# Seven products of quarters for eight in the first MLP product of a transformer block

## The chip, the cores and the metric

The kernel runs on one core of one Trainium2 chip. The metric is the device time of one execution in microseconds, the median of several runs; a profiled execution gives the span from the first to the last instruction and the work of every engine: TensorE (PE, with its weight loads PEld), VectorE (DVE), ScalarE (ACT), GpSimd (POOL) and SyncE (SP), which issues the DMA transfers.

## The reference

A residual block over 512 tokens of width 1024: a gated linear recurrence and a differential attention run side by side on the same normed input, are merged and projected, and an MLP of width 4096 with a squared ReLU follows. All data are fp32. What matters here is the end:

```python
x = x + merged @ w_out[l]
h2 = rms_norm(x, norm2_g[l])
x = x + jnp.square(jax.nn.relu(h2 @ w_mlp1[l])) @ w_mlp2[l]
return rms_norm(x, normf_g)
```

`rms_norm` divides every token by the root of its mean square plus 1e-6 and multiplies by a gain per channel. `w_mlp1` is 1024 x 4096, `w_mlp2` 4096 x 1024.

## The kernel before

Activations lie transposed: 128 channels on the partitions, 512 tokens along the free dimension, so that 1024 channels are eight tiles (index `k` or `m`). Each fp32 operand is split into a high part (a cast to fp32r, on ACT) and a low part (the remainder, on DVE). `Build.mm` makes one block of 128 output channels from 8 tiles of k, each with three matmuls (high by high, high by low, low by high; lines 153 to 155): 24 matmuls of 512 columns into one PSUM bank.

Weights come in chunks of 128 x 1024, two to a DMA of 1 MB (`raw`, two buffers, issued on SP). `chunk_plan` writes their order out. `Build.emit_chunk` splits a chunk (lines 117 and 118) into the buffers `whi` and `wlo`, four of each; `Build.chunk` keeps three to four chunks ahead. A program places the instructions in each engine's queue at compile time, by their order in the source and by when their inputs should be ready; each engine then runs its queue in order.

The stages: values and other input projections, with attention and recurrence between them; the merge; the output projection with the residual (eight blocks, line 620 adds the residual, line 231 splits x times gain into the next product's operands); norm 2 (`token_rinv` sums the squares over channels by matmuls with a column of ones, line 245, takes the root and the reciprocal; `bcast_rinv` spreads it over the partitions by matmuls with an identity, line 256); then the MLP by quarters of its width:

```python
    mlp1(0)
    for qq in range(NQ - 1):
        mlp1(qq + 1)
        mlp2(qq)
```

`mlp1` makes eight blocks of the first product. Line 639 reads each from PSUM, clips it at zero and multiplies by the token scale; line 644 squares it into the high part, lines 645 and 646 give the low part. `mlp2` makes eight blocks of the second product from one quarter and line 653 adds each to the residual. The last quarter of the second product runs by halves of the tokens (256 columns), and line 672 adds; the final norm of each half ends with line 683 and the output transfers.

## Time and profile before

| | us |
|---|---|
| median of 3 runs (lowest, highest) | 901.84 (901.81, 902.35) |
| span of the profiled execution | 900.2 |
| PE busy in the span | 888.8 |
| DVE busy | 510.7 |
| ACT busy | 395.3 |

The runs' times and the span come from different executions; the profiled execution's own device time is not given beside its span. PE's busy time counts overlapping matmuls once, and the ends of matmuls are modelled, so the price of a matmul is read from the distance of two starts rather than from a duration.

### The profile page before, as it was taken

To read this page: it belongs to the slowest core of one execution; us is meant where nothing else is said; L and a number is where in the kernel's file an instruction comes from. 1 tells how busy PE (TensorE), PEld (TensorE's weight loads), DVE (VectorE), ACT (ScalarE), POOL (GpSimd) and SP (SyncE) were. 2 spreads that over 40 slices of the span, in tenths; PEclk is the share of its full clock that TensorE was granted. 3 is DMA by queue.
4 is the path that set the end of the run, shared out by engine and by line. 5 is a ranking of instruction groups with operands and counts; after the bars stand their busy time and mean duration, and the time that the engine had idled before them with its cause. 6 is when DMAs were issued, how large, how long until landed. Compare 5 with 4: busy or idle time off the path is not lost.

```text
span 900.2 us, 10638 instructions
## 1 busy us (share of the span) xinstructions
PE 888.8 (99%) x4209; PEld 720.1 (80%) x4209; DVE 510.7 (57%) x796; ACT 395.3 (44%) x658; POOL 0.3 (0%) x5
## 2 busy tenths in 40 slices
PE   9999999999999999999999999999999999999995
PEld 7887787777877788888888888888888888888995
DVE  7777698787887765333334555555335534555332
ACT  7544767857858973222223342222122212223232
POOL 0000000000000000000000000000000000000000
PEclk9999999999999999999999999999999999999998
DMA  8433123132323022222522222222222222225011
GB/s 279 171 125 114 59 71 129 59 111 83 109 70 109 13 82 94 93 94 94 187 93 94 94 95 93 94 94 94 94 94 94 94 94 93 94 94 175 13 48 48
DMA packets 20738, 88.49 MB, mean 98 GB/s; under 512 B 3024, under 2 KB 6352, under 8 KB 11728
## 3 DMA queue, kind: packets, MB, share of 16 engines
q1 hardware_dynamic: 20688, 87.81, 28.6%
q8 instruction: 33, 0.54, 0.2%
q14 instruction: 17, 0.14, 0.0%
HBM read 81.51 MB, written 2.10 MB: 93 GB/s over the span
## 4 chain that ended last, share of the span: by engine, by line
PE 97%; ACT 1%; DVE 1%; DMA 1%; SPq 0%; issue 0%; DVEq 0%; ACTq 0%
PE pmm L153 29%; PE pmm L154 28%; PE pmm L155 28%; PE psc L320 2%; PE pmm L320 2%; PE psc L408 2%; PE pmm L443 2%; PE ptr L431 1%; DMA L<-xT 1%; PE psc L504 1%; PE psc L506 0%; PE ptr L472 0%; PE psc L505 0%; PE psc L405 0%; PE ptr L245 0%; PE ptr L256 0%
## 5 line engine op out<-in xcount | busy, mean ns | idle before, releaser
L117 ACT CAST whi<-raw 128x1024 fp32r<-128x1024 f32 (+1 forms) x136 | 139.3, 1025 | 373.6 <-PE pmm L154 298.9
L153 PE MATMUL pmm<-X,whi 128*128 128x512 f32 x584 | 232.9, 399 | 0.0
L154 PE MATMUL pmm<-X,whi 128*128 128x512 f32 x584 | 230.7, 395 | 0.0
L155 PE MATMUL pmm<-X,wlo 128*128 128x512 f32 x584 | 230.7, 395 | 0.0
L118 DVE TENSOR_TENSOR wlo<-raw,whi 128x1024 fp32r<-128x1024 f32 (+1 forms) x136 | 161.8, 1191 | 75.0 <-ACT whi L117 74.5
L153 PEld LDWEIGHTS pmm<-X,whi 128*128 128x128 f32 x584 | 109.9, 188 | 29.2 <-issue 2.6
L155 PEld LDWEIGHTS pmm<-X,wlo 128*128 128x128 f32 x584 | 109.9, 188 | 25.8
L154 PEld LDWEIGHTS pmm<-X,whi 128*128 128x128 f32 x584 | 109.9, 188 | 25.3 <-issue 0.4
L639 DVE SCALAR_TENSOR_TENSOR tmp<-pmm,up 128x512 f32<-128x512 f32 x32 | 22.1, 691 | 68.7 <-PE pmm L155 68.7
L653 DVE TENSOR_TENSOR E<-pmm,E 128x512 f32<-128x512 f32 x24 | 16.6, 691 | 74.7 <-PE pmm L155 74.7
L213 ACT ACTIVATE B<-psc,nb 128x128 f32<-128x128 f32 (+3 forms) x64 | 33.2, 523 | 27.1 <-DVE nb L413 27.0
L213 ACT ACT_TABLE_LOAD x32 | 41.1, 1283 | 1.1 <-DVE nb L413 0.5
L155 PE MATMUL pmm<-B,wlo 128*128 128x512 f32 x96 | 38.0, 395 | 0.0
L155 PE MATMUL pmm<-V,wlo 128*128 128x512 f32 x96 | 37.9, 395 | 0.0
L153 PE MATMUL pmm<-B,whi 128*128 128x512 f32 x96 | 37.9, 395 | 0.0
L153 PE MATMUL pmm<-V,whi 128*128 128x512 f32 x96 | 37.9, 395 | 0.0
L154 PE MATMUL pmm<-B,whi 128*128 128x512 f32 x96 | 37.9, 395 | 0.0
L154 PE MATMUL pmm<-V,whi 128*128 128x512 f32 x96 | 37.9, 395 | 0.0
L155 PE MATMUL pmm<-R,wlo 128*128 128x512 f32 (+1 forms) x96 | 34.2, 356 | 0.0
L155 PE MATMUL pmm<-Q,wlo 128*128 128x512 f32 (+1 forms) x96 | 34.2, 356 | 0.0
L154 PE MATMUL pmm<-R,whi 128*128 128x512 f32 (+1 forms) x96 | 34.2, 356 | 0.0
L154 PE MATMUL pmm<-Q,whi 128*128 128x512 f32 (+1 forms) x96 | 34.2, 356 | 0.0
(232 smaller groups left out, 1411.4 us busy)
## 6 DMA issues: line engine op xcount, KB each, us to landing
raw<-wts SPq DMA_DIRECT2D x70, 1024.0 KB, 4.8
rot<-B SPq DMA_DIRECT2D x64, 64.0 KB, 2.0
L<-xT SPq DMA_DIRECT2D x8, 256.0 KB, 5.3
raw<-wts SPq DMA_DIRECT2D x8, 256.0 KB, 5.4
E<-xT SPq DMA_DIRECT2D x8, 256.0 KB, 4.5
out<-E SPq DMA_DIRECT2D x6, 256.0 KB, 2.5
tmp<-gates SPq DMA_DIRECT2D x8, 128.0 KB, 4.7
out<-E SPq DMA_DIRECT2D x4, 128.0 KB, 1.9
```

The lines of the kernel that those rows point to most:

```text
L117: nc.scalar.copy(hf[:, s], raw[:, s])
L118: nc.vector.tensor_tensor(lf[:, s], raw[:, s], hf[:, s].bitcast(F), op=ALU.subtract)
L153: nc.tensor.matmul(ps, hi[:, k], xh[k], start=(k == 0), stop=False)
L154: nc.tensor.matmul(ps, hi[:, k], xl[k], start=False, stop=False)
L155: nc.tensor.matmul(ps, lo[:, k], xh[k], start=False, stop=(k == KT - 1))
L213: ins = A.activation(*args, **kw).ins
L320: TE.matmul(pvs[half][i], xs[q][:, i * P:(i + 1) * P], (hv, lv)[wi][:, q % 2], start=(q == 0 and n == 0), stop=(q == KT - 1 and n == 2))
L408: TE.matmul(sc[:, m, :n], l[rows, 0, i * P:n], r[rows, 1, :n], start=(g == 0), stop=(g == 2))
L431: TE.transpose(pt[:, j], p[:, j * P:(j + 1) * P], ident)
L443: TE.matmul(po[:, i], pdT[:, j], v[j][:, h * P:(h + 1) * P], start=(j == 0), stop=(j == i))
L639: V.scalar_tensor_tensor(z, pz, 0.0, rb2, op0=ALU.max, op1=ALU.mult)
L653: V.tensor_tensor(x2[m], pz, x2[m], op=ALU.add)
```

## The change

The first product is taken in units. A unit makes two blocks of 128 output channels that lie 512 apart, for all tokens, as a product of 2 x 2 quarters: the channels of the input in two halves, the tokens in two halves, the output channels in two blocks. Strassen's scheme in Winograd's form makes it from seven products of quarters instead of eight. Each is 4 tiles of k, three matmuls each, with 256 columns: 12 matmuls, 84 a unit, into four PSUM banks (`BX`, `BY`, `BR`, `BZ`), three of which take a second product on top of the first. The seven weight operands ("pieces" of 128 x 512) are the four quarters or their sums, made by DVE and then split by ACT and DVE; the seven activation operands are made once, in the output projection's loop. Since sums of quarters are taken over tokens and channels, the token scale of norm 2 no longer stands between product and ReLU: the operands carry only a scale from norm 1's sums (`isz`), the residual is multiplied by the rest (`sig2`) ahead of the second product, and the final norm's epsilon becomes one per token (`eps4`). The squares of norm 2 are added on GpSimd.

Weights of the MLP come in units of 1 MB, one for the seven pieces of a "one" unit (first product) or the four pieces of a "two" unit (two blocks of the second product, four tiles of k each). A ring of eight pieces takes the place of the four chunk buffers; `use` makes the piece seven ahead. `mlp_order` gives four "one" units of the first quarter, and then "one" of the next quarter and "two" of this one in turn. The last quarter's eight chunks are held as before. The output projection goes over its blocks in the order 0, 4, 1, 5, 2, 6, 3, 7. The core of the diff:

```diff
+def mlp_order():
+    order = [("one", 0, i) for i in range(4)]
     for q in range(NQ):
-        if q + 1 < NQ:
-            for f in range(8):
-                plan.append(("w_mlp1", ((q + 1) * 8 + f) * P, 0))
-        for m in range(KT):
-            plan.append(("w_mlp2", m * P, q * D))
-    return plan
+        for i in range(4):
+            if q + 1 < NQ:
+                order.append(("one", q + 1, i))
+            order.append(("two", q, i))
+    return order
...
+    RING = 8
+    def plan_pieces(self):
+        self.units = mlp_order()
+        self.pieces = []
+        self.first = []
+        for u, (kind, q, i) in enumerate(self.units):
+            self.first.append(len(self.pieces))
+            if kind == "one":
+                self.pieces += [(u, j) for j in range(7)]
+            elif q < NQ - 1:
+                self.pieces += [(u, j) for j in range(4)]
+        self.ring_h, self.ring_l = [], []
+        self.piece, self.made = {}, 0
+        self.raw_u = {}
+        self.sums = {}
+    def load_unit(self, u):
+        if u < len(self.units) and u not in self.raw_u:
+            raw = self.t("raw", (P, 4, T), bufs=2)
+            self.nc.sync.dma_start(raw.rearrange("p c f -> p (c f)"), self.a["wts"][self.mlp0 // 2 + u])
+            self.raw_u[u] = raw
+    def split_to(self, src, hi, lo):
+        self.nc.scalar.copy(hi, src)
+        self.nc.vector.tensor_tensor(lo, src, hi.bitcast(F), op=ALU.subtract)
+    def make_piece(self):
+        V, n = self.nc.vector, self.made
+        u, j = self.pieces[n]
+        self.load_unit(u)
+        self.load_unit(u + 1)
+        raw = self.raw_u[u]
+        blk = [raw[:, i] for i in range(4)]
+        if self.units[u][0] == "one":
+            if j == 0:
+                s1 = self.sums[u] = self.t("pT", (P, T))
+                V.tensor_tensor(s1, blk[2], blk[3], op=ALU.add)
+                V.tensor_tensor(blk[2], blk[2], blk[0], op=ALU.add)
+            elif j == 1:
+                V.tensor_tensor(blk[0], blk[0], self.sums[u], op=ALU.add)
+            elif j == 6:
+                V.tensor_tensor(blk[1], blk[1], blk[0], op=ALU.add)
+            src = (blk[0], blk[0], blk[2], self.sums[u], blk[1], blk[3], blk[1])[j]
+        else:
+            src = blk[j]
+        s, e = n // 2 % (self.RING // 2), n % 2
+        if n < self.RING and e == 0:
+            self.ring_h.append(self.t("whi", (P, 2, T), FR, bufs=4))
+            self.ring_l.append(self.t("wlo", (P, 2, T), FR, bufs=4))
+        hi, lo = self.ring_h[s][:, e], self.ring_l[s][:, e]
+        self.split_to(src, hi, lo)
+        self.piece[n] = [x.rearrange("p (k m) -> p k m", m=P) for x in (hi, lo)]
+        self.made += 1
+    def make_until(self, n):
+        while self.made < min(n, len(self.pieces)):
+            self.make_piece()
+    def use(self, n):
+        self.make_until(n + self.RING)
+        return self.piece.pop(n)
+    def mm4(self, out, w, xs, first, last):
+        nc = self.nc
+        for k, (xh, xl) in enumerate(xs):
+            for g, (l, r) in enumerate(((w[0], xh), (w[0], xl), (w[1], xh))):
+                nc.tensor.matmul(out, l[:, k], r, start=(first and k == 0 and g == 0),
+                                 stop=(last and k == 3 and g == 2), skip_group_check=True)
...
-    def token_rinv(parts, sl=range(4)):
+    def token_sums(parts, sl=range(4)):
         pc = ps("tr", (P, T))
         for i in sl:
             for n, sq in enumerate(parts):
                 TE.matmul(pc[:, i:i + 1], sq[:, i * P:(i + 1) * P], ones[:, 0:1],
                           start=(n == 0), stop=(n == len(parts) - 1))
-        r = t("rcol", (P, 4))
-        s = slice(sl[0], sl[-1] + 1)
-        act(r[:, s], pc[:, s], AF.Sqrt, scale=1.0 / D, bias=eps1)
-        V.reciprocal(r[:, s], r[:, s])
-        return r
+        return pc
...
-    # ---- residual and norm 2 ----
-    x2, x2p = [], []
-    x2h, x2l = [], []
+    b.plan_pieces()
+    isz = t("isz", (P, 4))
+    V.reciprocal(isz, size1)
+    r1b = t("up0")
+    bcast_rinv(isz, r1b)
+    x2, x2p = [None] * KT, [None] * (KT // 2)
+    th = [t(f"X{2 * k}", (P, 4, H2), FR) for k in range(4)]
+    tl = [t(f"X{2 * k + 1}", (P, 4, H2), FR) for k in range(4)]
+    b2h = [t(f"L{k}", (P, 2, T), FR) for k in range(2)]
+    b2l = [t(f"L{k + 2}", (P, 2, T), FR) for k in range(2)]
+    b1h, b1l = t("S0", (P, 4, H2), FR), t("S1", (P, 4, H2), FR)
     ssq = t("up1")
-    for m in range(KT):
-        if m % 2 == 0:
-            xp = t(f"E{m // 2}", (P, 2, T))
-            x2p.append(xp)
-        xk = xp[:, m % 2]
+    for n, m in enumerate(OUT_ORDER):
+        k = m % 4
+        if n > 4:
+            b.make_until(2 * (n - 4))
+        if x2p[m // 2] is None:
+            x2p[m // 2] = t(f"E{m // 2}", (P, 2, T))
+        xk = x2[m] = x2p[m // 2][:, m % 2]
         nc.sync.dma_start(xk, a["xT"][m])
         po = b.proj(mh, ml)
         V.tensor_tensor(xk, po, xk, op=ALU.add)
-        x2.append(xk)
-        hi, lo = pair(f"X{m}")
-        split_scaled(xk, col(C_G2, m), hi, lo)
-        x2h.append(hi)
-        x2l.append(lo)
-        add_squares(ssq, xk, m == 0)
-    rcol = token_rinv([ssq])
-    rb2 = t("up0")
-    bcast_rinv(rcol, rb2)
-    # ---- MLP ----
-    fq = {}
-    def mlp1(qq):
-        out = []
-        for f in range(8):
-            pz = b.proj(x2h, x2l)
-            z = t("tmp", bufs=2)
-            V.scalar_tensor_tensor(z, pz, 0.0, rb2, op0=ALU.max, op1=ALU.mult)
-            if qq % 2 == 0:
-                hi, lo = pair(f"V{f}" if f < 4 else f"B{f - 4}")
+        if m < 4:
+            xs = t(f"V{k}", (P, 2, T))
+        V.scalar_tensor_tensor(xs[:, m // 4], xk, col(C_G2, m), r1b, op0=ALU.mult, op1=ALU.mult)
+        if n == 0:
+            A.activation(ssq, xk, AF.Square)
+        else:
+            sq = t("tmp", bufs=2)
+            A.activation(sq, xk, AF.Square)
+            nc.gpsimd.tensor_tensor(ssq, ssq, sq, op=ALU.add)
+        if m >= 4:
+            q4 = xs.rearrange("p a (c f) -> p (a c) f", c=2)
+            b.split_to(q4[:, 0], b1h[:, k], b1l[:, k])
+            tt = t(f"B{k}", (P, 4, H2))
+            V.tensor_tensor(tt[:, 0:3:2], q4[:, 0:2], q4[:, 1:4:2], op=ALU.subtract)
+            V.tensor_tensor(tt[:, 1], tt[:, 0], q4[:, 3], op=ALU.add)
+            V.tensor_tensor(tt[:, 3], q4[:, 2], tt[:, 1], op=ALU.subtract)
+            b.split_to(tt, th[k], tl[k])
+            b.split_to(xs[:, 1], b2h[k // 2][:, k % 2], b2l[k // 2][:, k % 2])
+    b.make_until(b.RING)
+    pc = token_sums([ssq])
+    sig2 = t("sig2", (P, 4))
+    V.tensor_scalar(sig2, pc[:, :4], 1.0 / D, EPS, op0=ALU.mult, op1=ALU.add)
+    V.tensor_tensor(sig2, sig2, isz, op=ALU.mult)
+    V.tensor_tensor(sig2, sig2, isz, op=ALU.mult)
+    eps4 = t("eps4", (P, 4))
+    V.tensor_tensor(eps4, sig2, sig2, op=ALU.mult)
+    V.tensor_scalar(eps4, eps4, EPS, None, op0=ALU.mult)
+    sg2b = t("up0")
+    bcast_rinv(sig2, sg2b)
+    for xp in x2p:
+        V.tensor_tensor(xp, xp, sg2b.unsqueeze(1).to_broadcast([P, 2, T]), op=ALU.mult)
+    xc = {
+        "b11": [(b1h[:, k], b1l[:, k]) for k in range(4)],
+        "b21": [(b2h[k // 2][:, k % 2, :H2], b2l[k // 2][:, k % 2, :H2]) for k in range(4)],
+        "b22": [(b2h[k // 2][:, k % 2, H2:], b2l[k // 2][:, k % 2, H2:]) for k in range(4)],
+    }
+    for j in range(4):
+        xc[f"t{j + 1}"] = [(th[k][:, j], tl[k][:, j]) for k in range(4)]
+    banks = [ps("sc", (P, 2, T), bufs=2) for _ in range(2)]
+    BX, BY, BR, BZ = (banks[n // 2][:, n % 2, :H2] for n in range(4))
+    fq = {q: [None] * KT for q in range(NQ)}
+    def f_split(q, f, z, lo_half):
+        if q % 2 == 0:
+            hi, lo = pair(f"V{f}" if f < 4 else f"B{f - 4}")
+        else:
+            hi, lo = pair(f"R{f}" if f < 4 else f"Q{f - 4}")
+        A.activation(z[:, lo_half:], z[:, lo_half:], AF.Relu)
+        A.activation(hi, z, AF.Square)
+        A.activation(z, z, AF.Square)
+        V.tensor_tensor(lo, z, hi.bitcast(F), op=ALU.subtract)
+        fq[q][f] = (hi, lo)
...
+    def one(u, q, i):
+        n = b.first[u]
+        z0 = t("up2" if i % 2 == 0 else "rot", bufs=1 + i % 2)
+        z1 = t("up3" if i % 2 == 0 else "rot", bufs=1 + i % 2)
+        b.mm4(BX, b.use(n), xc["b11"], True, True)
+        uu = t("tmp", (P, H2), bufs=2)
+        A.copy(uu, BX)
+        b.mm4(BY, b.use(n + 1), xc["t2"], True, True)
+        V.tensor_tensor(uu, BY, uu, op=ALU.subtract)
+        b.mm4(BR, b.use(n + 2), xc["t3"], True, True)
+        V.tensor_tensor(z1[:, H2:], BR, uu, op=ALU.add)
+        b.mm4(BZ, b.use(n + 3), xc["t1"], True, True)
+        V.tensor_tensor(z1[:, H2:], z1[:, H2:], BZ, op=ALU.subtract)
+        b.mm4(BX, b.use(n + 4), xc["b21"], False, True)
+        A.activation(z0[:, :H2], BX, AF.Relu)
+        b.mm4(BR, b.use(n + 5), xc["t4"], False, True)
+        V.tensor_tensor(z1[:, :H2], BR, uu, op=ALU.add)
+        b.mm4(BZ, b.use(n + 6), xc["b22"], False, True)
+        V.tensor_tensor(z0[:, H2:], BZ, uu, op=ALU.subtract)
+        f_split(q, i + 4, z1, 0)
+        f_split(q, i, z0, H2)
+    def two(u, q, i):
+        n = b.first[u]
+        for c in range(2):
+            m = 2 * i + c
+            pz = ps("mm", bufs=3)
+            for h in range(2):
+                b.mm4(pz, b.use(n + 2 * c + h), fq[q][4 * h:4 * h + 4], h == 0, h == 1)
+            V.tensor_tensor(x2[m], pz, x2[m], op=ALU.add)
...
+    def hold(u, i):
+        b.load_unit(u)
+        b.load_unit(u + 1)
+        for c in range(2):
+            e = 2 * i + c
+            if e < 4:
+                hi, lo = t(f"X{2 * e}", (P, KT, P), FR), t(f"X{2 * e + 1}", (P, KT, P), FR)
             else:
-                hi, lo = pair(f"R{f}" if f < 4 else f"Q{f - 4}")
-            A.activation(hi, z, AF.Square)
-            V.tensor_tensor(z, z, z, op=ALU.mult)
-            V.tensor_tensor(lo, z, hi.bitcast(F), op=ALU.subtract)
-            out.append((hi, lo))
-        fq[qq] = ([o[0] for o in out], [o[1] for o in out])
-    def mlp2(qq):
-        for m in range(KT):
-            pz = b.proj(*fq[qq])
-            V.tensor_tensor(x2[m], pz, x2[m], op=ALU.add)
-    mlp1(0)
-    for qq in range(NQ - 1):
-        mlp1(qq + 1)
-        mlp2(qq)
-    # ---- last quarter, by halves of the tokens, and the final norm ----
-    wl = []
+                hi, lo = t("whi", (P, KT, P), FR, bufs=4), t("wlo", (P, KT, P), FR, bufs=4)
+            b.split_to(b.raw_u[u][:, 2 * c:2 * c + 2], *(x.rearrange("p (c k) m -> p c (k m)", c=2) for x in (hi, lo)))
+            last_chunks.append((hi, lo))
+    held = 0
+    for u, (kind, q, i) in enumerate(b.units):
+        if kind == "one":
+            one(u, q, i)
+        elif q < NQ - 1:
+            two(u, q, i)
+            if q == NQ - 2 and i >= 2:
+                hold(len(b.units) - 4 + held, held)
+                held += 1
+    while held < 4:
+        hold(len(b.units) - 4 + held, held)
+        held += 1
...
-        rcol = token_rinv([ssq, sq], tk)
+        c = slice(2 * half, 2 * half + 2)
+        pc = token_sums([ssq, sq], tk)
+        rcol = t("rcol", (P, 4))
+        V.scalar_tensor_tensor(rcol[:, c], pc[:, c], 1.0 / D, eps4[:, c], op0=ALU.mult, op1=ALU.add)
+        act(rcol[:, c], rcol[:, c], AF.Sqrt)
+        V.reciprocal(rcol[:, c], rcol[:, c])
```

## Rows read from the trace of the kernel before

**Rows 1.** The page, busy time of each engine, share and instructions.

```profile
PE 888.8 (99%) x4209; PEld 720.1 (80%) x4209; DVE 510.7 (57%) x796; ACT 395.3 (44%) x658; POOL 0.3 (0%) x5
```

**Rows 2.** The page, chain that ended last, by engine.

```profile
PE 97%; ACT 1%; DVE 1%; DMA 1%; SPq 0%; issue 0%; DVEq 0%; ACTq 0%
```

**Rows 3.** Windows: stretch, length, busy us per engine (instructions), TensorE clock, DMA.

```profile
483.10:528.00 44.90, 44.90 (x194) 36.07 (x193) 24.78 (x31) 17.10 (x24) 0.00 (x0) 1.00 0.26 94
528.00:842.50 314.50, 314.50 (x1360) 253.94 (x1359) 154.73 (x183) 83.28 (x97) 0.00 (x0) 1.00 0.28 97
842.50:889.20 46.70, 46.70 (x399) 46.62 (x398) 16.01 (x35) 15.24 (x32) 0.00 (x0) 1.00 0.07 24
889.20:900.20 11.00, 1.82 (x14) 1.46 (x12) 3.13 (x7) 1.19 (x3) 0.00 (x0) 0.69 0.29 96
```

**Rows 4.** Timeline, DVE, first product: start us, duration us, instruction [idle before].

```profile
602.55 0.69 DVE L639 SCALAR_TENSOR_TENSOR tmp<-pmm,up 128x512 f32<-128x512 f32 x1 [2.11 <-PE pmm L155]
603.45 1.23 DVE L118 TENSOR_TENSOR wlo<-raw,whi 128x1024 fp32r<-128x1024 f32 x1 [0.20 <-ACT whi L117]
604.59 0.69 DVE L645 TENSOR_TENSOR tmp<-tmp 128x512 f32<-128x512 f32 x1
605.31 0.69 DVE L646 TENSOR_TENSOR Q<-tmp,Q 128x512 fp32r<-128x512 f32 x1
608.13 0.69 DVE L639 SCALAR_TENSOR_TENSOR tmp<-pmm,up 128x512 f32<-128x512 f32 x1 [2.13 <-PE pmm L155]
```

**Rows 5.** Timeline, DVE, last quarter.

```profile
845.93 0.42 DVE L672 TENSOR_TENSOR E<-pmm,E 128x256 f32<-128x256 f32 x1 [0.73 <-PE pmm L155]
...
851.56 0.42 DVE L672 TENSOR_TENSOR E<-pmm,E 128x256 f32<-128x256 f32 x1 [1.48 <-PE pmm L155]
```

**Rows 6.** Groups, weight loads: busy us, mean ns | idle before.

```profile
L154 PEld LDWEIGHTS pmm<-X,whi 128*128 128x128 f32 x584 | 109.9, 188 | 25.3 <-issue 0.4
...
L153 PEld LDWEIGHTS pmm<-R,X 128*128 128x128 f32 x32 | 6.0, 188 | 0.0
```

**Rows 7.** Timeline, DVE, runs of unrelated operations in the value stage.

```profile
35.77 4.91 DVE L316 TENSOR_TENSOR L<-L,up 128x512 f32<-128x512 f32 x8 [0.59 <-ACT up L260]
...
43.45 3.39 DVE L231 SCALAR_TENSOR_TENSOR X<-L,small,X 128x512 fp32r<-128x512 f32 x5
```

**Rows 8.** Timeline, the end of the kernel, DVE.

```profile
891.49 0.17 DVE L250 RECIPROCAL rcol<-rcol 128x2 f32<-128x2 f32 x1 [1.66 <-ACT rcol L213]
...
892.46 2.54 DVE L683 TENSOR_TENSOR E<-E,ptr 128x256 f32<-128x256 f32 x5 [0.80 <-PE ptr L256]
```

**Rows 9.** Groups by form, ACT: busy us, mean ns | idle before.

```profile
L117 ACT CAST whi<-raw 128x1024 fp32r<-128x1024 f32 x128 | 134.5, 1051 | 373.5 <-PE pmm L154 298.9 <-issue 64.5 <-PE pmm L155 4.8
...
L674 ACT ACTIVATE tmp<-E 128x256 f32<-128x256 f32 x14 | 5.8, 418 | 24.5 <-DVE E L672 24.5
...
L644 ACT ACTIVATE V<-tmp 128x512 fp32r<-128x512 f32 x8 | 5.0, 628 | 1.0 <-DVE tmp L639 1.0
...
L117 ACT CAST whi<-raw 128x512 fp32r<-128x512 f32 x8 | 4.9, 606 | 0.1
```

**Rows 10.** Timeline, PE, after the output projection.

```profile
531.75 0.99 PE L245 MATMUL ptr<-ones,up 128*128 128x1 f32 x8
532.60 0.48 PE L154 MATMUL pmm<-X,whi 128*128 128x512 f32 x1
...
534.78 1.05 PE L256 MATMUL ptr<-ident,rcol 128*128 128x128 f32 x8
535.59 0.47 PE L154 MATMUL pmm<-X,whi 128*128 128x512 f32 x1
```

**Rows 11.** Timeline, DVE, end of the output projection.

```profile
522.63 0.69 DVE L620 TENSOR_TENSOR E<-pmm,E 128x512 f32<-128x512 f32 x1 [2.27 <-PE pmm L155]
...
528.23 0.69 DVE L620 TENSOR_TENSOR E<-pmm,E 128x512 f32<-128x512 f32 x1 [2.27 <-PE pmm L155]
```

**Rows 12.** The page, DMA issues: KB each, median us to landing.

```profile
raw<-wts SPq DMA_DIRECT2D x70, 1024.0 KB, 4.8
```

More of the change, by code (lines that the diff above doesn't have):

```diff
@@ L34 @@
 NSMALL = 89
+OUT_ORDER = (0, 4, 1, 5, 2, 6, 3, 7)
+H2 = T // 2
 def chunk_plan():
@@ L52, in chunk_plan @@
             plan.append((kind, m * P, 0))
-    for m in range(KT):
+    for m in OUT_ORDER:
         plan.append(("w_out", m * P, 0))
-    for f in range(8):
-        plan.append(("w_mlp1", f * P, 0))
-    for q in range(NQ):
-        if q + 1 < NQ:
-            for f in range(8):
-                plan.append(("w_mlp1", ((q + 1) * 8 + f) * P, 0))
-        for m in range(KT):
-            plan.append(("w_mlp2", m * P, q * D))
-    return plan
+    for kind, q, i in mlp_order():
+        if kind == "one":
+            for f in (i, i + 4):
+                plan.append(("w_mlp1", (q * 8 + f) * P, 0))
+        else:
+            for m in (2 * i, 2 * i + 1):
+                plan.append(("w_mlp2", m * P, q * D))
+    return plan
+def mlp_order():
+    order = [("one", 0, i) for i in range(4)]
+    for q in range(NQ):
+        for i in range(4):
[3 more added lines that the diff above has]
+    return order
 def merge_order():
@@ L82, in __init__ @@
         self.nchunks = len(chunk_plan())
+        self.mlp0 = self.nchunks - 2 * len(mlp_order())
         self.split = {}
@@ L127, in wslot @@
             return "E0", "E1", 1
-        e = c - (self.nchunks - 8)
-        if 0 <= e < 4:
-            return f"X{2 * e}", f"X{2 * e + 1}", 1
         return "whi", "wlo", 4
@@ L136, in chunk @@
         ahead = 4 if c + 4 < self.P1_END else 3
-        if c >= self.nchunks - 8 - 4:
-            ahead = 7
-        while self.emitted < min(c + 1 + ahead, self.nchunks):
+        while self.emitted < min(c + 1 + ahead, self.mlp0):
             self.emit_chunk(self.emitted)
@@ L193, in block_kernel @@
     nc.sync.dma_start(ident, a["ident"])
+    size1 = t("size1", (P, 4))
     ones = t("ones", (P, 1))
@@ L308, in block_kernel @@
                 if half == 1 and k == 1:
-                    rcol = token_rinv([ssq])
+                    pc = token_sums([ssq])
+                    rcol = t("rcol", (P, 4))
+                    act(rcol, pc[:, :4], AF.Sqrt, scale=1.0 / D, bias=eps1)
+                    V.reciprocal(rcol, rcol)
+                    act(size1, pc[:, :4], AF.Sqrt, scale=1.0 / D, bias=ones)
                     v_store(0)
@@ L650, in mlp2 @@
-    def mlp2(qq):
-        for m in range(KT):
-            pz = b.proj(*fq[qq])
-            V.tensor_tensor(x2[m], pz, x2[m], op=ALU.add)
-    mlp1(0)
-    for qq in range(NQ - 1):
-        mlp1(qq + 1)
-        mlp2(qq)
-    wl = []
+        if m < 4:
[7 more added lines that the diff above has]
+            nc.gpsimd.tensor_tensor(ssq, ssq, sq, op=ALU.add)
@@ new lines, in block_kernel @@
+    b.make_until(b.RING)
+    pc = token_sums([ssq])
+    sig2 = t("sig2", (P, 4))
[9 more added lines that the diff above has]
+        V.tensor_tensor(xp, xp, sg2b.unsqueeze(1).to_broadcast([P, 2, T]), op=ALU.mult)
@@ new lines, in f_split @@
+    def f_split(q, f, z, lo_half):
+        if q % 2 == 0:
+            hi, lo = pair(f"V{f}" if f < 4 else f"B{f - 4}")
+        else:
+            hi, lo = pair(f"R{f}" if f < 4 else f"Q{f - 4}")
[25 more added lines that the diff above has]
+        f_split(q, i, z0, H2)
@@ L662, in block_kernel @@
+    held = 0
+    for u, (kind, q, i) in enumerate(b.units):
+        if kind == "one":
+            one(u, q, i)
[7 more added lines that the diff above has]
+        held += 1
     ssq = t("up1")
-    fh, fl = fq[NQ - 1]
-    H2 = T // 2
     for half in range(2):
@@ L667, in block_kernel @@
         for m in range(KT):
-            if half == 0:
-                wl.append(b.next())
+            hi, lo = last_chunks[m]
             pz = ps("mm", bufs=3)
-            b.mm(pz[:, s], wl[m], [f[:, s] for f in fh], [f[:, s] for f in fl])
+            for h in range(2):
+                b.mm4(pz[:, s], (hi[:, 4 * h:4 * h + 4], lo[:, 4 * h:4 * h + 4]),
+                      [(fh[:, s], fl[:, s]) for fh, fl in fq[NQ - 1][4 * h:4 * h + 4]], h == 0, h == 1)
             V.tensor_tensor(x2[m][:, s], pz[:, s], x2[m][:, s], op=ALU.add)
```

4 lines of the change are left out of this document (2 added, 2 removed).

## The prediction

> **What bounds the kernel now.** I read the busy totals first: TensorE (PE) is busy for 99% of the span, VectorE (DVE) for 57%, ScalarE (ACT) for 44% [rows 1]. A busy total alone can mislead where matmuls overlap, so the chain of waits comes second: 97% of what ended last is PE work [rows 2]. Third come the stages [rows 3]. Output projection, first and second product together, and last quarter have no PE gap, at a granted clock of 1.00 (the 2.4 GHz level). The middle stage, 528.0 to 842.5 us, holds the first product and three quarters of the second. DVE works for 154.7 of its 314.5 us. So PE time saved there shortens the kernel, as long as DVE and ACT can feed and empty the new products.
>
> PE's price is read from its readers' rhythm. In the first product the reader of each block starts at 602.55 and 608.13: 24 matmuls of 512 columns in 5.58 us, 0.2325 each [rows 4]. In the last quarter readers start at 845.93 and 851.56 with one between: 48 matmuls of 256 columns in 5.63 us, 0.1173 each [rows 5]. Half the columns cost half the time, plus 1%. This settles whether half-width products can pay at all.
>
> **The change part by part, on PE.** Before, two blocks of the first product are 48 matmuls: 48 x 0.2325 = 11.16 us. After, the same two blocks are seven products of 12 matmuls with 256 columns: 84 x 0.1173 = 9.85. The saving is 1.31 us a unit, over 16 units 20.9 us. The second product keeps 24 matmuls of 512 columns per block and the last quarter its 384 of 256. Added is one broadcast of the per-token scale, as long as the one in the trace, 534.78 to 535.59: **+0.8** [rows 10]. The token sums and the other broadcast stay.
>
> **Weights on DVE and ACT.** A "one" unit makes seven pieces of 512 columns. Its DVE work is 7 subtractions, 4 sums, 5 PSUM reads of 256 and 2 subtractions for f: 13 operations of 512 and 5 of 256. Eight unrelated operations of 512 took 4.91 us, the last one 0.69 in full: 0.60 from start to start [rows 7]. For 1024 it is 1.14 (603.45 to 604.59) [rows 4]. Five at the end took 2.54, of which two of 256 come to 0.33 each [rows 8]. The unit is 13 x 0.60 + 5 x 0.33 = 9.45 us of DVE beside 9.85 of PE. A "two" unit asks DVE for 6 x 0.60 = 3.6 beside 48 x 0.2325 = 11.16. So a pair is 13.05 of 21.0, and the eight-piece ring has the whole "two" unit to refill. I take **+0.5** for the 12 pairs; the bounds are 0 and 7 (one operation of 0.6 late in each).
>
> ACT, at full durations: 7 casts of 0.61, 5 operations of 0.63 and 3 of 0.42 make 8.7 us a unit [rows 9]. It is hidden under PE's 9.85; in the stretch below that cover is thin.
>
> **The stretch with no "two" unit.** The order begins with five "one" units. Here DVE has no slack, and leftovers come first. From the end of the output projection until the fifth unit's last piece is made, DVE must do: the last chunk's add, scale and split (0.60 + 0.66 + 0.33 + 0.60 + 0.33 + 0.33 + 1.14 + 0.60 = 4.6; the scaled operation is 0.66 of 3.39 for five [rows 7]); pieces 6 and 7 with three sums, 3.0; the token factors, 5 small ones at about 0.2, 1.0; the residual's scaling, 4 x 1.14 = 4.6; 41 operations for pieces 8 to 34, 24.6; four units' results, 4 x 2.85 = 11.4; the fifth's first three reads, 1.0. Sum 50.2 us. With 0.2 until DVE starts (last matmul at about 528.0, reader at 528.23 [rows 11]) and the last piece's 12 matmuls, 1.4, PE ends at 51.8. PE's own work is 5 x 9.85 + 0.85 + 0.81 = 50.9 [rows 10]. The least wait is 0.9 us.
>
> The upper bound comes from related neighbours: an operation that reads what the one before it wrote starts after 0.72, not 0.60 [rows 4]. If all paid these 0.12 (58 of 512 elements, 26 of 256, 5 of 1024), 10.7 us come on top: 11.6. Few neighbours here feed each other, since each subtraction waits for an ACT cast made earlier; but waits for ACT and PE join in. I take **+4.0**, about a third of the way.
>
> Eight unrelated operations start every 0.60 while each lasts 0.69 [rows 7]. The Trainium skill, "VectorE: DVE Perf Modes", section "The DRAIN you can't avoid", has the next operation start only when the last has emptied, save where it is not held back; were all held back, the wait would be the 11.6 instead of 4.0. The trace shows such a spacing only for operations that feed each other, 0.72 [rows 4].
>
> PE's start is inside this. The last operand's chain is 0.2 + 0.69 + 0.74 + 0.60 + 0.33 + 0.33 + 1.05 + 1.23 = 5.2 us. The other three k tiles of the first product in each of four banks give 36 matmuls, 4.2 us of cover, if PE's order is filled as in the trace, where token sums sit inside a product [rows 10]. Without filling, some 2.6 us are lost, partly under the same DVE time.
>
> **What I cost at nothing.** The output projection's added DVE work: a pair of steps asks at most 10.1 us (7.6 where pieces 0 and 1 begin, then 2.5), PE gives 2 x 5.6 [rows 11]. Without that cover its rest would join the stretch. The GpSimd adds of squares: no GpSimd elementwise row exists; from below it is DVE's 0.69, from above even eight times that, 5.5, still fits the 5.6 us of a step [rows 11], and I take about 1.5, nearest to DVE's row; the last one is late only for the residual's scaling, which nobody reads before the first "two" unit. DMA moves the same megabytes in the same 1 MB transfers, 4.8 us each [rows 12]; SyncE's queue holds a load until a raw buffer is free, and a raw buffer is freed about a unit (10 us) before its next pieces are wanted. The last eight chunks split during the final "two" unit: 4.6 us of DVE for the first four in 11.2. At the end one small DVE operation joins a path that has nothing beside it: **+0.2**, from the reciprocal's 0.17 [rows 8].
>
> Sum: 900.2 - 20.9 + 0.8 + 0.5 + 4.0 + 0.2 = 884.8 us of span. The profiled execution's own time is not given beside its span; the median of the runs, 901.84, lies 1.64 above it, so the forecast is **886.4 us**.
>
> **The rivals.** *DVE sets the five-unit stretch at full price:* wait 11.6 for 4.0, so 894.0. For it: 9.45 of DVE against 9.85 of PE leaves nothing to hide a late operation. Against it: eight in a row did start every 0.60 [rows 7].
>
> *Slower, by the hand-over of two PSUM banks:* BR's second product (piece 5) waits until DVE has read its first (piece 2), and BZ's (6) likewise (3). Two pieces lie between, 24 x 0.1173 = 2.8 us; reading takes 0.2 + 0.42, so 2.2 us of DVE queue in front is free. To end above 903.6 us, 21.7 us must go, 1.36 in each of 16 units: a queue of 3.6 us, six operations of 512, ahead of the read in every unit. If the queue is eight (4.8), each unit loses 2.6, 41 us in all: about 924. For it: DVE runs in order, and weight work stands between the reads. Against it: in the pairs DVE has 38% free.
>
> *Weight loads bind at half width,* one after the other: 1344 x 0.188 = 252.7 us [rows 6] for the 768 x 0.2325 = 178.6 of before, 74 longer, about 976. The last quarter's 0.1173 speaks against it. The Trainium skill, "TensorE: Matmul & The Clock Gate", section "The mechanism", says that a load overlaps running matmuls only where their row groups differ, and here all use 128 rows; by that rule loads would not be hidden (another of its sections lets a load go to a background buffer). The trace disagrees: loads of 0.188 us stand beside a matmul every 0.1173 us, so they overlap [rows 5, 6].
>
> *Little change:* the pairs' upper bound of 7 and the stretch's 11.6 together leave about 900 (881.9 + 18.6).
>
> **How the numbers follow.** The median moved within 0.06% over three runs, so 0.2% (1.8 us) tells a change. Forecast, 882 to 891: 0.62. Stretch at full price, 891 to 896: 0.18. No waits at all, under 882: 0.05. Pairs late too, 896 to 900: 0.03; within 0.2%: 0.03. Hand-over, slower: 0.08; weight loads, slower: 0.01. Faster is 0.62 + 0.18 + 0.05 + 0.03 = 0.88, same 0.03, slower 0.09. The low end, 881.5, is a sum without any wait (900.2 - 20.9 + 1.0 + 1.64 = 881.9, and a little); the high end, 895.5, is the full-price stretch with 2 us in the pairs.
>
> **What would show it.** Matmuls of the "one" units every 0.117 us; 84 in 9.9 us in the pairs; no PE idle of over 0.3 us there. In the first 55 us after the output projection: DVE over 90% busy, PE with a few us of idle, ended by weight pieces or PSUM reads. The end from the last matmul on 0.2 us longer. Wrong it is if PE waits in the pairs too (hand-over), or if the stretch lasts over 57 us.

## The result, and the profile after

The changed kernel takes **908.89 us** (median of 4 runs, 907.9 to 909.69) against 901.83 for the kernel before on the same chip: a ratio of 1.0078, interval [1.0064, 1.0092]. It is slower, by 0.8%. The forecast was 886.4, in a range of 881.5 to 895.5. The profiled execution's span is 906.9 us. Every time given is a median of runs at the usual granted clock; one run of one version, at 1427.7 us and a clock of 0.557, is left out.

The page of the changed kernel, busy totals and the chain that ended last:

```profile
PE 885.7 (98%) x4793; PEld 741.9 (82%) x4793; DVE 597.1 (66%) x1008; ACT 477.5 (53%) x863; POOL 11.7 (1%) x12
...
PE 92%; DVE 5%; ACT 2%; issue 1%; POOLq 0%; DVEq 0%; ACTq 0%
```

PE's busy time fell by only 3.1 us [rows 1], and 8% of the chain is now other than PE work, for 3% before [rows 2]. The windows of the changed kernel say where (columns as in [rows 3]): the output projection, the stretch of the five units that have no "two" unit between them, and 240 us of the pairs.

```profile
483.10:529.10 46.00, 46.00 (x206) 37.89 (x205) 36.88 (x48) 18.50 (x27) 8.78 (x5) 1.00 0.20 69
529.10:590.00 60.90, 49.21 (x336) 45.95 (x335) 52.05 (x87) 32.06 (x62) 2.59 (x2) 0.86 0.20 70
600.00:840.00 240.00, 240.00 (x1476) 210.29 (x1476) 159.01 (x266) 115.73 (x212) 0.00 (x0) 1.00 0.29 101
```

The second row is the loss: PE works for 49.21 of 60.90 us at a mean granted clock of 0.86. Since the clock has two levels, 1.2 and 2.4 GHz, that is (1 - 0.86) x 2 x 60.9 = 17 us at the lower one. Before, no stretch of the MLP had either [rows 3]. The trace has these 17 us in two pieces, and PE starts 35 and 19 matmuls in them:

```profile
532.71:542.95 10.24, 8.19 (x35) 7.60 (x36) 9.72 (x19) 4.11 (x7) 1.32 (x1) 0.50 0.29 102
546.36:553.19 6.83, 4.19 (x19) 4.19 (x20) 5.79 (x9) 0.50 (x1) 0.00 (x0) 0.50 0.00 0
```

PE's busy time hides waits shorter than a matmul's pipeline. So I also use an **excess**: for each two neighbouring matmuls in the trace, the distance of their starts less the price of the first (0.2328 us for 512 columns, 0.1172 for 256, about 0.10 for the few short ones of the sums and the broadcast), summed over a stretch. It is 22.3 us from 520 to 600 us, where I had forecast 4.0, and 5.5 from 600 to 840, the pairs, where I had forecast 0.5. The price of a matmul went as forecast. Twelve matmuls of 256 columns take 1.41 us, 0.1175 each, as in [rows 5]; here the first, the last and the next product of a timeline of PE, columns start, duration, instruction:

```profile
656.93 0.40 PE L237 MATMUL psc<-S,whi 128*128 128x256 f32 x2
...
658.23 0.28 PE L237 MATMUL psc<-S,wlo 128*128 128x256 f32 x1
658.34 0.28 PE L237 MATMUL psc<-X,whi 128*128 128x256 f32 x1
```

**Three things in the trace of the stretch.** First, DVE operations beside a GpSimd add. From the changed kernel's timeline, DVE and POOL together (L719 reads a block of the output projection from PSUM, as L620 did in [rows 11]; L722 scales it; L728 adds squares):

```profile
516.87 1.87 DVE L722 SCALAR_TENSOR_TENSOR V<-E,small,up 128x512 f32<-128x512 f32 x1
516.89 1.30 POOL L728 TENSOR_TENSOR up<-up,tmp 128x512 f32<-128x512 f32 x1 [4.22 <-ACT tmp L727]
...
522.77 0.75 DVE L722 SCALAR_TENSOR_TENSOR V<-E,small,up 128x512 f32<-128x512 f32 x1
523.12 1.54 POOL L728 TENSOR_TENSOR up<-up,tmp 128x512 f32<-128x512 f32 x1 [4.94 <-ACT tmp L727]
523.43 1.78 DVE L193 TENSOR_TENSOR wlo<-pT,whi 128x512 fp32r<-128x512 f32 x1
...
529.95 1.83 DVE L722 SCALAR_TENSOR_TENSOR V<-E,small,up 128x512 f32<-128x512 f32 x1
529.97 1.27 POOL L728 TENSOR_TENSOR up<-up,tmp 128x512 f32<-128x512 f32 x1 [5.30 <-ACT tmp L727]
...
533.85 0.68 DVE L719 TENSOR_TENSOR E<-pmm,E 128x512 f32<-128x512 f32 x1
```

The same operation L722 takes 0.75 us alone and 1.83 or 1.87 beside an add. In the three places the lengthened operation ends 0.54 to 0.55 us after the add does (531.24 and 531.78 in the last): the DVE operation does its work once GpSimd is done. Each of the seven adds lengthens one DVE operation by about 1.1 us, and the last block of the output projection is read at 533.85, 4.7 us after its product (PE has begun the next stage at 529.13). Before, that read came at 528.23, with DVE waiting for it [rows 11].

Second, the residual's scaling. From the timeline of the changed kernel, DVE and PE:

```profile
532.28 0.38 PE L237 MATMUL psc<-S,whi 128*128 128x256 f32 x1 [1.93 <-ACT S L192]
...
543.98 4.63 DVE L752 TENSOR_TENSOR E<-E,up 128x1024 f32<-128x1024 f32 x4 [1.35 <-ACT up L340]
548.53 0.41 DVE L787 TENSOR_TENSOR tmp<-psc,tmp 128x256 f32<-128x256 f32 x1
549.00 0.80 PE L237 MATMUL psc<-L,whi 128*128 128x256 f32 x2 [4.97 <-DVE tmp L787]
...
553.09 0.45 PE L237 MATMUL psc<-L,whi 128*128 128x256 f32 x2
```

The four operations of the scaling stand in DVE's queue ahead of the read of `BY` (L787), and a product of PE waits 4.97 us for that read. What follows is dear as well: 18 matmuls take 4.09 us from 549.00 to 553.09, 0.227 each for 0.117, 2 us more, at the lower clock.

Third, the list of PE's waits from 520 to 600 us, in the changed kernel (us in total, times, longest):

```profile
PE psc L237 <- DVE tmp L787: 7.1, 4, 5.0
PE psc L237 <- ACT S L192: 1.9, 1, 1.9
PE psc L237 <- ACT tmp L785: 1.0, 1, 1.0
```

L785 is ACT's copy of `BX`, L787 DVE's read of `BY`. The product that waits for L787 four times is that with `b21` (operands `L`), and it writes `BX`. It waits for the read of *another* bank. So it goes in the pairs too:

```profile
615.74 0.37 ACT L785 COPY tmp<-psc 128x256 f32<-128x256 f32 x1
615.84 0.71 PE L237 MATMUL psc<-X,whi 128*128 128x256 f32 x3
616.15 0.30 PEld L237 LDWEIGHTS psc<-X,whi 128*128 128x128 f32 x2
...
617.94 0.42 DVE L787 TENSOR_TENSOR tmp<-psc,tmp 128x256 f32<-128x256 f32 x1 [0.29 <-PE psc L237]
618.14 0.40 PE L237 MATMUL pmm<-V,whi 128*128 128x512 f32 x1
618.42 0.30 PEld L237 LDWEIGHTS psc<-L,whi 128*128 128x128 f32 x2 [0.21 <-DVE tmp L787]
618.42 0.51 PE L237 MATMUL psc<-L,whi 128*128 128x256 f32 x2
```

The order of PE's instructions in the built program names the buffers and the engines whose signals an instruction waits for: `psc_866` holds `BX` and `BY`, `psc_867` `BR` and `BZ`. After the first product (operands `S`) come eight matmuls into `BR`, the twelve into `BY`, and later `b21` into `BX`:

```
2972 L237 MATMUL psc_867_4450<-X0_794_4055,whi_857_4415 128x256 [waits DVE_49,Activation_49]
...
2980 L237 MATMUL psc_866_4449<-X0_794_4055,whi_857_4415 128x256 [waits Activation_49]
...
2997 L237 MATMUL psc_866_4449<-L0_802_4063,whi_841_4280 128x256 [waits DVE_49]
```

The load that starts at 616.15 is that of the first matmul into `BY`, just behind the end of the copy of `BX` (615.74 + 0.37 = 616.11). At 618.42 the product into `BX` starts behind the read of `BY` (618.36). Where a load has waited like this, it starts together with its matmul instead of under the one in front, and the distance is 0.19 to 0.23 us for 0.117. Each pair has five such places, some 0.5 us in all.

The end behaves as forecast up to the final multiplication: 3.57 us from the last matmul's start (897.16) to it, against 3.37 before (889.09 to 892.46 in [rows 8]), the +0.2 of the sum.

```profile
897.16 0.28 PE L237 MATMUL pmm<-Q,wlo 128*128 128x256 f32 x1
...
900.73 2.54 DVE L864 TENSOR_TENSOR E<-E,ptr 128x256 f32<-128x256 f32 x5 [0.86 <-PE ptr L336]
```

From there to the end of the span it is 6.2 us for 7.7 before; why the output is faster by 1.5 us stays open.

### The profile page after: what moved, and what is told of

Its sections match the earlier page's. It is cut to its first block, busy times and chain, and to the rows that moved or that the text cites. A ratio compares the mean times of both kernels' runs of the same rounds, so it can differ in the third digit from the quotient of the medians.

```text
span 906.9 us, 12306 instructions
## 1 busy us (share of the span) xinstructions
PE 885.7 (98%) x4793; PEld 741.9 (82%) x4793; DVE 597.1 (66%) x1008; ACT 477.5 (53%) x863; POOL 11.7 (1%) x12
## 4 chain that ended last, share of the span: by engine, by line
PE 92%; DVE 5%; ACT 2%; issue 1%; POOLq 0%; DVEq 0%; ACTq 0%
PE pmm L237 20%; PE psc L237 17%; PE pmm L163 14%; PE pmm L165 14%; PE pmm L164 14%; PE pmm L405 3%; PE psc L405 2%; PE psc L493 2%; PE pmm L528 2%; PE ptr L516 1%; DVE wlo L193 1%; DVE V L722 1%; PE psc L589 1%; ACT whi L192 1%; PE ptr L336 1%
## 5 line engine op out<-in xcount | busy, mean ns | idle before, releaser
L192 ACT CAST whi<-raw 128x512 fp32r<-128x512 f32 (+1 forms) x148 | 90.5, 629 | 135.6 <-PE psc L237 59.3
L132 ACT CAST whi<-raw 128x1024 fp32r<-128x1024 f32 (+1 forms) x76 | 76.3, 1006 | 130.9 <-PE pmm L164 121.4
L163 PE MATMUL pmm<-X,whi 128*128 128x512 f32 x328 | 132.4, 404 | 0.0
L164 PE MATMUL pmm<-X,whi 128*128 128x512 f32 x328 | 130.1, 397 | 0.0
L165 PE MATMUL pmm<-X,wlo 128*128 128x512 f32 x328 | 130.0, 396 | 0.0
L133 DVE TENSOR_TENSOR wlo<-raw,whi 128x1024 fp32r<-128x1024 f32 (+1 forms) x76 | 89.5, 1179 | 60.0 <-ACT whi L132 59.4
L193 DVE TENSOR_TENSOR wlo<-raw,whi 128x512 fp32r<-128x512 f32 (+1 forms) x148 | 103.7, 709 | 33.3 <-ACT whi L192 30.7
L237 PE MATMUL psc<-X,whi 128*128 128x256 f32 x512 | 99.2, 292 | 1.7 <-ACT tmp L785 1.0
L237 PEld LDWEIGHTS psc<-X,whi 128*128 128x128 f32 x512 | 81.3, 194 | 7.6 <-DVE rot L791 2.0
L163 PEld LDWEIGHTS pmm<-X,whi 128*128 128x128 f32 x328 | 61.7, 188 | 18.1 <-issue 2.6
L164 PEld LDWEIGHTS pmm<-X,whi 128*128 128x128 f32 x328 | 61.8, 188 | 14.3 <-issue 0.4
L237 PE MATMUL psc<-X,wlo 128*128 128x256 f32 x256 | 71.4, 286 | 0.0
```

Of the source, the lines that this page charges most:

```text
L132: nc.scalar.copy(hf[:, s], raw[:, s])
L133: nc.vector.tensor_tensor(lf[:, s], raw[:, s], hf[:, s].bitcast(F), op=ALU.subtract)
L163: nc.tensor.matmul(ps, hi[:, k], xh[k], start=(k == 0), stop=False)
L164: nc.tensor.matmul(ps, hi[:, k], xl[k], start=False, stop=False)
L165: nc.tensor.matmul(ps, lo[:, k], xh[k], start=False, stop=(k == KT - 1))
L192: self.nc.scalar.copy(hi, src)
```

## The experiments

The first theory was that GpSimd and the place of the residual's scaling cost the time; its rival was the clock's fall by itself. When these two edits left 11 us unexplained, the theory became that the PSUM banks hang together by pairs.

**Squares on DVE.**

```diff
-            nc.gpsimd.tensor_tensor(ssq, ssq, sq, op=ALU.add)
+            V.tensor_tensor(ssq, ssq, sq, op=ALU.add)
```

> The squares of norm 2 are added on DVE instead of GpSimd, nothing else. Theory: in the changed kernel each of the seven GpSimd adds lengthens the DVE operation beside it by 1.1 us (0.68 to 1.78 and the like), and so DVE enters the first product some 4.5 us late. On DVE an add costs 0.6. DVE gains 7 x 0.5 = 3.5 us before the first product, no DVE operation of 512 lasts over 0.8 us there, and the time falls by 3 to 6 us, to 903 to 906. Rival, that PE's first wait comes from the last operand's chain and not from a backlog: the time stays within 1 us of 908.9.

Measured 898.6 us, ratio to before 0.9965 [0.9952, 0.9978]: 10.3 us less than the changed kernel, more than expected. Seven DVE operations of 0.69 were added, and no operation of the output projection is longer than it is alone. The granted clock of the stretch, 0.86 in the changed kernel, rises to 0.94, so the gain holds some of the clock too.

**The residual scaled late**, each pair of blocks just ahead of the "two" unit that first adds to it.

```diff
-    for xp in x2p:
-        V.tensor_tensor(xp, xp, sg2b.unsqueeze(1).to_broadcast([P, 2, T]), op=ALU.mult)
+    def scale_residual(i):
+        V.tensor_tensor(x2p[i], x2p[i], sg2b.unsqueeze(1).to_broadcast([P, 2, T]), op=ALU.mult)
...
         elif q < NQ - 1:
+            if q == 0:
+                scale_residual(i)
             two(u, q, i)
```

> The residual's four scalings stand in front of the four 'two' units that read them, instead of ahead of the first 'one' unit. Theory: PE's wait of 4.97 us at 544 to 549 us goes, and with it the second stretch of halved clock (6.8 us, in which 3 us are lost): 6 to 9 us less, 900 to 903. Rival, that DVE's total work sets the five-unit stretch whatever the order: 4.6 us of DVE work leave the stretch and no more than that is won, about 904; if the scalings have to be done in the pairs at PE's cost, 909.

Measured 902.8 us, 1.0012 [1.0003, 1.0022]: 6.1 less, as expected.

**Both.**

> Both of the other two edits: squares on DVE, scalings late. Theory: the gains add and the clock stays at its upper level through the stretch: 10 to 14 us less, 895 to 899, that is faster than before. Rival, DVE's total work alone: 3.5 + 4.6 = 8 us less, 901.

Measured 897.51 us, 0.9953 [0.9939, 0.9968]. Faster than the kernel before, but still 11 us above the forecast, with 10.8 us of excess from 520 to 600 and an unchanged 5.5 in the pairs. The clock did not stay at its upper level as expected (0.97 in the stretch). The two gains don't add up (10.3 + 6.1, together 11.4): something else still holds PE.

**PE kept at work in the gaps**, to test the clock: on the changed kernel, 24 and 20 matmuls of 512 columns without use.

```diff
+    def fill(count):
+        pf = ps("mm", bufs=3)
+        for _ in range(count):
+            TE.matmul(pf, b1h[:, 0, :P], b2h[0][:, 0], start=True, stop=True)
...
     pc = token_sums([ssq])
+    fill(24)
...
+        if u == 0:
+            fill(20)
```

> The changed kernel with 44 matmuls of 512 columns added whose result nobody reads: 24 ahead of the first product (5.6 us) and 20 between the first passes and the second pass of the first unit (4.7 us), about where PE waits. Output unchanged. Theory, that the fallen clock has a price of its own (about 6 us): the clock stays at 1.00 in the stretch and the time is 0 to 5 us lower in spite of 10 us more PE work. Rival, that DVE alone paces the stretch: clock 1.00 too, but the time stays within 1 us; and if PE's own work sets it, 10 us more.

Measured 911.98 us, 1.0114 [1.0097, 1.0131]: 3.1 more for 10.2 us of added matmuls. None of the three expected outcomes came. The lower clock did not go away but came once, for 6.8 us, so the run doesn't say what the clock costs by itself. It is inconclusive.

**Four buffers for the four banks.** In the changed kernel `BX` and `BY` are the two banks of one buffer, `BR` and `BZ` those of another.

```diff
-    banks = [ps("sc", (P, 2, T), bufs=2) for _ in range(2)]
-    BX, BY, BR, BZ = (banks[n // 2][:, n % 2, :H2] for n in range(4))
+    BY, BR = (ps("sc", (P, 2, T), bufs=2)[:, 0, :H2] for _ in range(2))
...
     def one(u, q, i):
+        BX, BZ = (ps("mm", bufs=3)[:, :H2] for _ in range(2))
```

> The changed kernel with one thing altered: the four PSUM banks of a unit belong to four buffers of the program instead of two buffers of two banks (BX and BZ now come from the three buffers of the second product). Theory (in a two-bank buffer a product into one bank waits for the read of the other bank: BY's for ACT's copy of BX, BX's second for DVE's read of BY, and so on, and the weight load of a product that waits is not made under the matmul in front): the distances of 0.19 to 0.23 between matmuls of 256 columns go from the pairs, 12 pairs fall from 21.5 to about 21.1 us (-5 to -6), and the units at 555 to 590 us lose part of their idle; 898 to 904 us. Rival (the reads of the same bank are what is waited for, by DVE's queue): pairs stay at 21.5 us and the time within 1 us of 908.9.

Measured 893.96 us, 0.9911 [0.9896, 0.9926]: 14.9 us less than the changed kernel, more than the theory's 5 to 11. In the pairs the excess is gone (-0.9 us; a negative sum means that the prices are a hair too high), and no place from 590 to 700 us is left with a distance over price + 0.05.

**Four buffers, squares on DVE, late scaling.**

> The same separate buffers on top of the version with the squares added on DVE and the residual scaled late (897.5 us). Theory: the pairs give 5 to 6 us and the stretch of five units 1 to 3; 888.5 to 891.5 us. Rival: within 1 us of 897.5.

Measured **881.0 us**, 0.9771 [0.9757, 0.9786]; it beats both kernels, and is 7.5 us under the lower end of what was expected: the pairs gave the 5 to 6 us (excess from 5.5 to -0.8), but the stretch gave 10 instead of 1 to 3 (10.8 to 0.9). Windows of this version:

```profile
529.10:590.00 60.90, 60.86 (x476) 58.76 (x475) 59.59 (x111) 42.19 (x84) 0.00 (x0) 1.00 0.30 105
600.00:840.00 240.00, 240.00 (x1536) 217.35 (x1535) 155.28 (x261) 117.67 (x213) 0.00 (x0) 1.00 0.29 101
```

In the same 60.9 us PE now makes 476 matmuls for 336, at a clock of 1.00, beside a DVE that is busy for 59.59 us. PE's list of waits from 520 to 600 us is empty, and the chain that ended last is 99% PE.

**Each alone on top of the four buffers.**

> The changed kernel with separate PSUM buffers and the squares added on DVE; the residual's scaling stays in front. It says what the scaling costs once the banks are separate (against 881.0 with all three). Theory (four operations of 1.22 us stand in DVE's queue before a PSUM read; PE waits for that read once, without them the wait is gone): 3 to 6 us above 881.0, so 884 to 887. Rival (with separate buffers no product waits for that read any more): 880.5 to 882.

> The changed kernel with separate PSUM buffers and late scaling; the squares are still added on GpSimd. It says what GpSimd costs by itself (against 881.0). Theory (seven DVE operations 1.1 us longer, and a last sum that comes late, less seven DVE adds of 0.6): 6 to 10 us above 881.0, so 887 to 891. Rival (most of the 10.3 us that the move to DVE gave was lost in waits between banks): 881 to 884.

With squares on DVE, 885.78 us, 0.9824 [0.9809, 0.9838]: the scaling in front costs 4.8. With late scaling, 889.05 us, 0.9862 [0.9845, 0.9878]: GpSimd costs 8.1. Here the two add up: from 894.0 the squares' move gains 8.2 and the late scaling 4.9, and 894.0 - 8.2 - 4.9 = 880.9. In the version with squares on DVE the read behind the scaling stands so (timelines of DVE and PE):

```profile
540.37 4.63 DVE L752 TENSOR_TENSOR E<-E,up 128x1024 f32<-128x1024 f32 x4
544.91 0.41 DVE L791 TENSOR_TENSOR up<-up,pmm 128x256 f32<-128x256 f32 x1
...
545.38 0.51 PE L237 MATMUL pmm<-L,whi 128*128 128x256 f32 x2 [1.05 <-DVE up L791]
...
552.78 0.48 PE L237 MATMUL psc<-X,whi 128*128 128x256 f32 x2 [1.70 <-DVE tmp L787]
```

PE does not wait once, as expected, but again at the next unit's read of `BY`, and 3.4 us at the lower clock follow (from 554.20). DVE is busy for 56.94 us of 529.10 to 590.00, so it has 4 us to spare in the stretch as a whole: the four operations cost time by where they stand, and moved back, in the 881.0 us version, they are done without a wait of PE.

In the version with four buffers and late scaling, PE waits for GpSimd's last sum as well, ahead of the token sums that stand in its own queue:

```profile
537.15 1.87 PE L329 MATMUL ptr<-ones,up 128*128 128x1 f32 x8 [2.62 <-POOL up L728]
```

**Twice the adds on GpSimd**, on the changed kernel; the second goes into a spare buffer.

```diff
             nc.gpsimd.tensor_tensor(ssq, ssq, sq, op=ALU.add)
+            spare = t("up2") if n == 1 else spare
+            nc.gpsimd.tensor_tensor(spare, sq, sq, op=ALU.add)
```

> The changed kernel, in which GpSimd makes each of its seven adds of squares and behind it one more add of the same size into a spare buffer (output unchanged). Theory (a DVE operation beside a GpSimd add lasts about 1.1 us longer): DVE has up to 7.7 us more work in the output projection, of which what falls before the last block is partly hidden; 912 to 918 us, and about twice as many DVE operations of 1.7 to 2.4 us in the output projection. Rival (what cost was GpSimd's own lateness, a wait for its last sum): 910 to 912 us and DVE operations as long as before.

Measured 913.62 us, 1.0136 [1.0119, 1.0153]: 4.7 more. Of the DVE operations from 490 to 560 us, 14 are lengthened, where the changed kernel has 7, one for each add. From its timeline:

```profile
519.41 1.87 DVE L722 SCALAR_TENSOR_TENSOR V<-E,small,up 128x512 f32<-128x512 f32 x1
519.43 1.30 POOL L728 TENSOR_TENSOR up<-up,tmp 128x512 f32<-128x512 f32 x1 [3.62 <-ACT tmp L727]
520.68 1.49 POOL L730 TENSOR_TENSOR up<-tmp 128x512 f32<-128x512 f32 x1
521.20 1.52 DVE L193 TENSOR_TENSOR wlo<-raw,whi 128x512 fp32r<-128x512 f32 x1
```

The subtraction L193, 0.68 alone, ends at 522.72, 0.55 behind the second add.

**Columns instead of buffers:** squares on DVE and late scaling, with units taking the left and right 256 columns of the banks in turn.

```diff
-    BX, BY, BR, BZ = (banks[n // 2][:, n % 2, :H2] for n in range(4))
...
+        BX, BY, BR, BZ = (banks[e // 2][:, e % 2, (u if u < 4 else u // 2) % 2 * H2:][:, :H2] for e in range(4))
```

> The version with squares on DVE and late scaling (897.5 us), still with two buffers of two banks each, but units take the left and the right 256 columns of the banks in turn. It parts two readings of what the separate buffers gave. Theory (a write waits for the reads of the whole two-bank buffer, whichever bank or half they touch): nothing changes, 897.5 within 1 us, distances of 0.19 to 0.23 us stay in the pairs. Rival (what helped was that the next unit's products go to other columns than those that the last unit's reads still hold): the separation by columns does the same, 881 to 890 us.

Measured 897.7 us, 0.9957 [0.9943, 0.9972], against 897.51 without: nothing changes.

**Four buffers without rotation:** the 881.0 us version, with one pair of buffers for `BX` and `BZ` in the first four units.

```diff
+    xz = []
     def one(u, q, i):
...
-        BX, BZ = (ps("mm", bufs=3)[:, :H2] for _ in range(2))
+        if u == 0 or u >= 4:
+            xz[:] = [ps("mm", bufs=3)[:, :H2] for _ in range(2)]
+        BX, BZ = xz
```

> The version with all three alterations (881.0 us), but its first four units use one and the same pair of buffers for BX and BZ; from the fifth unit on these two rotate again. It tells the separation of the four banks from the rotation that came with it. Theory (what cost was that a product into one bank waited for a read of another): the stretch of the first units keeps its 0.9 us of excess, or up to 2; 881 to 882.5 us. Rival (what helped there was that a unit's first products don't wait for the reads of the unit before in the same bank): the excess of the stretch goes towards the 10.8 us that it had with shared buffers, 886 to 891 us.

Measured 882.17 us, 0.9786 [0.977, 0.9802]. In the first units rotation gives 1.2 us; the other 8.6 us by which the excess of the stretch falls (10.8 to 2.2) are the separation. In the pairs the buffers rotate in this version too; that the 6.3 us there (5.5 to -0.8) come from the separation is read from the waits for another bank, and not tested apart. One wait appears, of the kind that one expects, for a read of the bank itself:

```profile
PE pmm L237 <- ACT up L797: 1.0, 1, 1.0
```

The versions side by side; excess as above, and the mean granted clock from 529.10 to 590.00 us:

| version | us | excess 520 to 600 | clock | excess 600 to 840 |
|---|---|---|---|---|
| changed kernel | 908.9 | 22.3 | 0.86 | 5.5 |
| late scaling | 902.8 | 16.5 | 0.92 | 5.4 |
| squares on DVE | 898.6 | 12.7 | 0.94 | 5.5 |
| both | 897.5 | 10.8 | 0.97 | 5.5 |
| both, halves of banks in turn | 897.7 | 11.2 | 0.97 | 5.3 |
| four buffers | 894.0 | 12.3 | 0.92 | -0.9 |
| four buffers, late scaling | 889.1 | 8.8 | 0.94 | -0.9 |
| four buffers, squares on DVE | 885.8 | 6.2 | 0.97 | -0.8 |
| all three, no rotation at first | 882.2 | 2.2 | 1.00 | -0.8 |
| all three | 881.0 | 0.9 | 1.00 | -0.8 |

The clock rises as the waits go, so a gain in the stretch holds a part of the clock's price wherever the two clocks differ.

## Why the prediction was wrong

**The saving was right.** From the MLP's first matmul to its last, the kernel before takes 361.1 us (528.03 to 889.09) and the 881.0 us version 340.1 (528.98 to 869.03): 21.0 less, for -20.9 in the sum. The added broadcast stands ahead of the output projection (484.13), and the MLP begins 0.95 later, for +0.8. The price 0.1173 held, weight loads did not bind, and the way from the last matmul to the final multiplication grew by 0.2.

**DVE's work was near the sum too.** In the changed kernel DVE works for 49.4 us from the last block's read (533.85) to the end of the fifth unit's last weight piece (592.11, the 35th split since the first piece), for 50.2 in the sum; but it takes 58.3 us for it:

```profile
533.85:592.11 58.26, 49.21 (x343) 46.39 (x343) 49.41 (x85) 31.60 (x60) 1.32 (x1) 0.86 0.21 73
```

The fair test of the +4.0 is the version with four buffers and squares on DVE, which keeps the scaling where the prediction had it: 6.2 us of excess, of which about 1.5 are matmuls at the lower clock. The 881.0 us version is not the kernel of the forecast: its scaling no longer stands in front. That it comes out at the case "no waits at all" (881.9, with 0.05) is in part luck, since 1.5 us of it are the faster output, which the sum did not have.

**First failed step: "The GpSimd adds of squares" at nothing.** Their own duration was near the estimate (1.27 to 2.26 us for about 1.5), but that was the wrong question. They hold DVE: 8.1 us by themselves, 10.3 in the changed kernel, with what follows from it (a last block read 4.7 us late, PE's waits for the last operand, some of the lower clock). The step's cover, "fits the 5.6 us of a step", spoke of GpSimd's own queue alone. The Trainium skill, "SBUF — State Buffer", section "SBUF: two separate sides", says that DVE and GpSimd share a pair of ports as an exclusive lock, which also a DVE operation with two SBUF inputs needs against a GpSimd operation that reads SBUF; whoever starts first has it for the whole instruction. The trace agrees: one lengthened operation for each add, ending 0.55 us behind it (1.08 for the one of 1024 columns), and the two adds of 2.2 us are those that begin while a DVE operation of 1024 columns runs. Only on who starts first it is not clean: two of the seven blocked operations start 0.02 us ahead of their add (516.87 and 516.89). The prediction did not look there. It also held that the last sum is late only for the residual's scaling; but the token sums in PE's own queue read it first, and PE waits 2.62 us for it in the version with four buffers and late scaling, 0.4 in the changed kernel.

**Second failed step: the hand-over of PSUM banks, a rival with 0.08.** It weighed waits for a read of the same bank (`BR`, `BZ`), with 2.2 us of slack, and a queue of six operations as the point from which it decides. No such queue was needed. The waits go by the buffer, so that `BY` waits for `BX`'s copy, `BX` for `BY`'s read, and likewise `BR` and `BZ`, with no slack to speak of: 14.9 us in the changed kernel, 16.5 once the other two were mended. That columns in turn change nothing and separate buffers nearly everything shows it. The waits come from the program, not from the chip: separate banks ran without them. The Trainium skill, "PSUM — Partial Sum Buffer", section "PSUM bank collisions raise a hardware error", asks only for two engines to stay off one bank at a time and has accesses to different banks run clean; the version with four buffers agrees, with -0.9 us of excess in the pairs.

**Third failed step: the residual's scaling as 4.6 us of DVE work alone.** As work it was in the sum, where it mattered little: without it DVE would be done at 47.2, ahead of PE's 50.9, so by the sum it costs no more than the least wait of 0.9. As a block in DVE's queue it stands ahead of reads that PE waits for: 4.8 us with four buffers, 6.1 in the changed kernel. The prediction called the scaling something "which nobody reads before the first "two" unit", and did not ask what is queued behind it.

**The terms.** +0.5 for the pairs measured 5.5, inside its bounds of 0 to 7, but not for the reason given (a late DVE operation in each); that the bounds held is luck. +4.0 for the stretch measured 22.3; its upper bound of 11.6 was one of DVE's spacing and held none of the three. Nothing in the sum stood for the clock, which was at the lower level for 17 us of the changed kernel's stretch and never in that of the 881.0 us version. Its own share can be bounded, as an estimate: PE starts 54 matmuls in those 17 us, and one costs about 0.11 us more there (0.227 for 0.117), so the lower clock made at most some 6 of the 22.3 us. The rest is waits. Two signs named ahead came: PE waits in the pairs, and a stretch of over 57 us (the fifth unit's last piece is ready at 592.11, 63 us after the stretch began).
